# The causal mask of a scan's decays: loaded from DRAM under an adding load, in place of a select on GpSimd over each group's tile

## The chip, the cores and the metric

The kernel runs on one core of one Trainium2 chip. The metric is the time of one execution on the device in microseconds (us). A core has a matrix engine (PE, with its weight loads shown apart as PEld), a vector engine (DVE), a scalar engine (ACT), GpSimd (POOL), and a queue engine without arithmetic (SP). Each engine works through its own list of instructions in order, and an instruction waits on semaphores for what others must have done before it. Loads and stores (DMAs) are issued by SP, ACT or POOL and carried out by 16 DMA engines that they share.

## The reference

One block of a network on 512 tokens of width 1024: an RMS norm, one wide projection, a convolution branch, a state-space branch, gates, an output projection, and a feed-forward part. The change lies in the state-space branch, in the weights by which a token reads earlier ones:

```
a_dt = dt * a                                  # per head, per token
a_cs = cumsum(a_dt)                            # running sums within a chunk
seg  = a_cs[l] - a_cs[s]
decay_in = exp(where(s <= l, seg, -inf))       # causal
cb   = einsum(c_mat, b_mat)                    # per group, l by s
y_diag = einsum(cb, decay_in, x * dt)
```

There are 8 groups of 4 heads (32 heads of width 64). The reference takes chunks of 64 tokens; the kernel works with chunks of 128, so it has 4 chunks, and a group's decays are a tile of 128 partitions (s) by 4 heads x 4 chunks x 128 tokens (l) in float32: 128 x 2048, 1 MB.

## The kernel before

Every large matrix product is made of three float32r passes (`mm3`: high by high, low by high, high by low part), so each strip of weights of 128 x 1024 is loaded (`w_raw`, L194, on SP's queue, tile `raw`), cast to a high part (`w_part`, L202, ACT, `whi`), and given a low part `wlo` in one of two ways: DVE subtracts (L209), or ACT writes the negated high part (L206) and POOL's queue issues an adding load of the same weights onto it (L207, `accum_op=ADD`). Five `raw` and five `whi`/`wlo` buffers exist, so that a strip is loaded several strips ahead of the products that use it.

The state-space branch is a loop over the 8 groups. Iteration g projects x, B and C of group g (`px`, `pB`, `pC` in three banks taken in turn), runs their short convolutions on ACT and DVE (L599, L601, L605), and between these products carries out the scan of group g-1 in steps:

- `s1(g-1)` transposes, scales by dt (`xdt`, L670), and multiplies the decays by C B (L686, DVE, in place in tile `L`)
- `s2(g-1)` makes the states (`pSa`, `pSb`, then `prev`, L698 to L701) and the within-chunk outputs `yd` (L709: 64 small products that read `L`)
- `s3(g-1)` adds the part from earlier chunks (`pYa`, `pYb`, L721), the gate and the norm (L717 to L748)
- `s4` transposes back for the output projection `pso`, whose first four strips' results ACT copies out (L780) and later ones DVE adds up (L782)

Between these, DVE works through the taps of a long convolution (L514, tile `a`; ACT starts each channel block of it, L511), a number of them per step.

Tile `L` of group g+1 is made at the end of iteration g (`make_L`). The running sums of all heads lie in a DRAM tile `scr`; POOL's queue loads the group's 4 x 4 x 128 sums to all 128 partitions (L486, a plain load of 1 MB), POOL's `affine_select` puts -1e30 where l < s (L489), and 16 exponentials on ACT, one per head and chunk with the negated running sum of s as bias, turn it into decays (L496). `L` has two buffers. Group g+1 takes that of group g-1, so its load waits until the products `yd` of group g-1 are done.

A scheduler orders each engine's list from the order of the code and the dependences. Loads of weights keep their order among themselves, and `by_table` keeps the exponentials and the other users of a table of functions in order on ACT.

Of the kernel before, what the change touches and what calls it, by code (L numbers as in the profile page):

```python
# [18 lines left out]
P = 128  # L19
T = 512  # L20
NT = T // P
# [5 lines left out]
G = 8  # L27
HG = H // G
# [142 lines left out]
def block_kernel(ctx: ExitStack, tc: tile.TileContext, x, xT, x0, prm, hp, gp, wf, w, out):  # L171
    nc = tc.nc
# [258 lines left out]
    dec = ssd.tile([P, NT, H], F32, name="dec")  # L431
    cd = ssd.tile([P, NT, H], F32, name="cd")
    scr = dr.tile([H, NT, P], F32, name="scr")

    scratch = ssd.tile([P, 8, CH], F32, tag="y", bufs=2, name="scratch")
    ta, tb, tcx, td, acs, acsT, te = (scratch[:, i, :].rearrange("p (a b) -> p a b", a=NT) for i in range(7))
# [39 lines left out]
    def by_table(ins):  # L476

        if "table" in mark:
            not_before(ins, mark["table"])
        mark["table"] = ins  # L480

    def make_L(g, first=None):
        L = ssd.tile([P, HG, NT, P], F32, tag="L", bufs=2, name=f"L{g}")
        Lf = L.rearrange("p h c l -> p (h c l)")
        src = scr[HG * g : HG * (g + 1)].rearrange("h c l -> (h c l)").partition_broadcast(P)
        load = pool.dma_start(Lf, src)  # L486
        if first:
            not_before(load, first)
        pool.affine_select(  # L489
            out=Lf, in_=Lf, compare_op=ALU.is_ge, fill=-1e30, base=0,  # L490
            pattern=[[0, HG * NT], [1, P]], channel_multiplier=-1,
        )
        for c in range(NT):
            for h in range(HG):
                by_table(
                    act.activation(L[:, h, c, :], L[:, h, c, :], AF.Exp, bias=nacs[:, c, HG * g + h : HG * g + h + 1])  # L496
                )
        return L


    vs, va, taps = [], [], []
# [18 lines left out]
    st = {}  # L520
# [29 lines left out]
    for j in range(NK):  # L550
        if j == EARLY:
            proj_z0()
            time_steps()
        if j == DT2:
            running_sums()
            L = {0: make_L(0)}
        if j == 0:
            three = [glu_tile(n) for n in ("pv0", "pg0", "pv1")]
            ws = [w_get("val", 0), w_get("glu", 0), w_get("val", 1)]
            for k in range(NK):  # L560
                c = slice(k * P, (k + 1) * P)
                for n in range(6 if k < 2 else 3):
                    ps, (wh, wl) = three[n % 3], ws[n % 3]
                    if n < 3:
                        in_order(pe.matmul(ps, wh[:, c], ehi[k], start=k == 0, stop=False))
                        in_order(pe.matmul(ps, wl[:, c], ehi[k], start=False, stop=False))
                    if k > 1 or n > 2:
                        mark["pe"] = in_order(pe.matmul(ps, wh[:, c], elo[k], start=False, stop=k == NK - 1))
            continue
        early = (ehi, elo) if j < EARLY else None  # L570
        pv = three[2] if j == 1 else glu_tile(f"pv{j}")
        if j == 2:
            proj(pv, w_get("val", j), early, slice(0, 3))
            norm_to_all()
            gated(0, *three[:2], True)
            gated(1, *first, True)
            proj(pv, w_get("val", j), early, slice(3, NK))
        elif j > 1:
            proj(pv, w_get("val", j), early)
        pg = glu_tile(f"pg{j}")  # L580
        if j == 1:
            proj(pg, w_get("glu", j), early, slice(0, 4))
            with tc.issue_after(mark["pe"].ins):
                norm_x()
            proj(pg, w_get("glu", j), early, slice(4, NK))
# [199 lines left out]
    for g in range(G):  # L785
        proj_x(g, 0)
        proj_x(g, 1)
        if g % 2 and g > 1:
            s4(g - 2)
        if g:  # L790
            s1(g - 1)
        conv_some((TAPS[g] + 0) // 5 + (TAPS[g] + 1) // 5)
        st[g]["L"] = L.pop(g)
        proj_bc(g, "B")
        if g % 2 and g > 1:
            ssm_out((g - 3) // 2, (0, 1))
        if g:
            s2(g - 1)
        if g % 2 == 0 and g > 1:
            s4(g - 2)  # L800
        conv_some((TAPS[g] + 2) // 5)
        proj_bc(g, "C")
        if g % 2 and g > 1:
            ssm_out((g - 3) // 2, (2, 3))
        if g:
            s3(g - 1)
        conv_some((TAPS[g] + 3) // 5)
        if g == 1:
            proj_z1()
        if g and g % 2 == 0:  # L810
            proj_zz(g)
        if g + 1 < G:
            L[g + 1] = make_L(g + 1, st.pop("lo", None))
        conv_some((TAPS[g] + 4) // 5)


# [986 lines left out]
```

## Time and profile before

| | |
|---|---|
| median of 3 runs | 1017.24 us (1017.21 to 1019.05) |
| span of the profiled execution, first to last instruction | 1016.0 us |
| the median less that span: what lies around it | 1.2 us |
| PE busy | 1007.7 us, 99% of the span |
| DVE, ACT, POOL busy | 847.9, 616.9, 106.7 us |
| moved by DMAs | 155.02 MB, mean 153 GB/s |
| loads of `L` | 8 of 1024 KB, median 7.6 us from issue to landing |
| selects on `L` | 8, some 2.0 us each |

Busy time is the union of the intervals in which an engine had an instruction in flight; matmuls overlap, so a busy PE says that it had no gap, not that each product was quick. The share in brackets is of the span. In the rows by group or in order of time, a bracket at the end holds the engine's idle time just before the row and what ended it; L with a number is a line of the kernel, `out<-in` the tiles written and read.

### The profile page before, as it was taken

To read this page: it belongs to the slowest core of one execution; us is meant where nothing else is said; L and a number is where in the kernel's file an instruction comes from. 1 tells how busy PE (TensorE), PEld (TensorE's weight loads), DVE (VectorE), ACT (ScalarE), POOL (GpSimd) and SP (SyncE) were. 2 spreads that over 40 slices of the span, in tenths; PEclk is the share of its full clock that TensorE was granted. 3 is DMA by queue.
4 is the path that set the end of the run, shared out by engine and by line. 5 is a ranking of instruction groups with operands and counts; after the bars stand their busy time and mean duration, and the time that the engine had idled before them with its cause. 6 is when DMAs were issued, how large, how long until landed. Compare 5 with 4: busy or idle time off the path is not lost.

```text
span 1016.0 us, 15943 instructions
## 1 busy us (share of the span) xinstructions
PE 1007.7 (99%) x6184; PEld 881.7 (87%) x6184; DVE 847.9 (83%) x1233; ACT 616.9 (61%) x1038; POOL 106.7 (11%) x138
## 2 busy tenths in 40 slices
PE   9999999999999999999999999999999999999997
PEld 7898889888888888888888889889999999998886
DVE  7899977868696879678987889788999887899974
ACT  7655775667666746573552685466666566568552
POOL 0101202120121011100110111012000000001001
PEclk9999999999999999999999999999999999999999
DMA  8567635645554465356452355624755555469622
GB/s 302 151 168 218 158 96 145 187 110 144 158 151 117 130 182 151 102 135 163 99 139 69 114 142 165 223 104 118 230 151 160 153 143 146 128 177 295 212 83 83
DMA packets 43803, 155.02 MB, mean 153 GB/s; under 512 B 5072, under 2 KB 6096, under 8 KB 42704
## 3 DMA queue, kind: packets, MB, share of 16 engines
q1 hardware_dynamic: 30672, 105.44, 30.7%
q0 software_dynamic: 11136, 43.00, 21.7%
q10 hardware_dynamic: 1920, 5.57, 1.6%
q8 instruction: 48, 0.79, 0.3%
q14 instruction: 27, 0.22, 0.1%
HBM read 149.73 MB, written 4.26 MB: 152 GB/s over the span
## 4 chain that ended last, share of the span: by engine, by line
PE 87%; DVE 8%; ACT 3%; issue 1%; DMA 1%; SPq 0%; POOL 0%; POOLq 0%; DVEq 0%; ACTq 0%
PE xy L246 4%; PE xy L252 4%; PE xy L248 4%; PE pso L246 3%; PE pso L248 3%; PE pso L252 3%; PE yv L246 2%; PE yv L252 2%; PE yv L248 2%; PE px L246 2%; PE px L252 2%; PE px L248 2%; DVE a L514 2%; PE pz L248 2%; PE pz L252 2%; PE pz L246 2%
## 5 line engine op out<-in xcount | busy, mean ns | idle before, releaser
L514 DVE SCALAR_TENSOR_TENSOR a<-v,prm_t,a 128x511 f32<-128x511 f32 (+15 forms) x240 | 183.8, 769 | 14.3 <-ACT a L511 12.3
L202 ACT CAST whi<-raw 128x1024 fp32r<-128x1024 f32 x99 | 102.6, 1048 | 127.9 <-PE pso L248 36.7
L209 DVE TENSOR_TENSOR wlo<-raw,whi 128x1024 fp32r<-128x1024 f32 x58 | 70.6, 1220 | 32.7 <-ACT whi L202 32.5
L207 POOL DMA_DIRECT2D wlo<-in_w x41 | 36.5, 891 | 369.1 <-ACT wlo L206 171.4
L248 PE MATMUL pz<-wlo,hhi 128*128 128x512 f32 (+2 forms) x160 | 56.2, 351 | 0.2
L252 PE MATMUL pz<-whi,hlo 128*128 128x512 f32 (+2 forms) x160 | 56.1, 352 | 0.0
L246 PE MATMUL pz<-whi,hhi 128*128 128x512 f32 (+2 forms) x160 | 55.4, 353 | 0.0
L246 PE MATMUL px<-hhi,whi 128*128 128x512 f32 x128 | 50.2, 392 | 0.0
L246 PE MATMUL pso<-yh,whi 128*128 128x512 f32 x128 | 50.2, 394 | 0.0
L252 PE MATMUL px<-hhi,wlo 128*128 128x512 f32 x128 | 49.8, 389 | 0.0
L248 PE MATMUL px<-hlo,whi 128*128 128x512 f32 x128 | 49.8, 389 | 0.0
L248 PE MATMUL pso<-yl,whi 128*128 128x512 f32 x128 | 49.8, 390 | 0.0
L252 PE MATMUL pso<-yh,wlo 128*128 128x512 f32 x128 | 49.7, 390 | 0.0
L1189 ACT CAST whi_g<-raw 128x1024 fp32r<-128x1024 f32 x40 | 41.2, 1052 | 10.6 <-PE yv L248 4.9
L601 DVE SCALAR_TENSOR_TENSOR x<-px,prm_t,x 128x511 f32<-128x511 f32 (+2 forms) x48 | 34.7, 743 | 13.9 <-ACT x L599 13.8
L1196 DVE TENSOR_TENSOR wlo_g<-raw,whi_g 128x1024 fp32r<-128x1024 f32 x34 | 41.3, 1221 | 3.5 <-ACT whi_g L1189 3.4
L206 ACT ACTIVATE wlo<-whi 128x1024 fp32r<-128x1024 f32 x41 | 43.3, 1055 | 0.3
L496 ACT ACTIVATE L<-L,nacs 128x128 f32<-128x128 f32 x128 | 38.8, 389 | 0.1
L248 PEld LDWEIGHTS pz<-wlo,hhi 128*128 128x128 f32 x160 | 30.1, 188 | 4.9 <-DVE wlo L209 1.0
L246 PEld LDWEIGHTS pz<-whi,hhi 128*128 128x128 f32 x160 | 30.2, 189 | 3.9
L252 PEld LDWEIGHTS pz<-whi,hlo 128*128 128x128 f32 x160 | 30.1, 188 | 3.7
L1189 ACT CAST chi_g<-raw 128x1024 fp32r<-128x1024 f32 x24 | 24.9, 1053 | 8.8 <-PE yv L248 3.4
(763 smaller groups left out, 3450.7 us busy)
## 6 DMA issues: line engine op xcount, KB each, us to landing
raw<-in_w SPq DMA_DIRECT2D x182, 512.0 KB, 4.5
wlo<-in_w POOLq DMA_DIRECT2D x41, 512.0 KB, 6.8
L<-scr POOLq DMA_DIRECT2D x8, 1024.0 KB, 7.6
wlo_g<-in_w POOLq DMA_DIRECT2D x11, 512.0 KB, 7.0
clo_g<-in_w POOLq DMA_DIRECT2D x6, 512.0 KB, 5.5
pws<-in_w POOLq DMA_DIRECT2D x8, 256.0 KB, 5.9
pw_raws<-in_w SPq DMA_DIRECT2D x4, 512.0 KB, 7.0
xr<-in_x ACTq DMA_DIRECT2D x4, 512.0 KB, 3.9
```

Source lines behind the costliest of these rows:

```text
L202: mark[n, c.start] = act.copy(hi[:, c], src)
L206: act.activation(lo[:, c], hi[:, c].bitcast(F32), AF.Copy, scale=-1.0)
L207: mark["lo"] = pool.dma_start(lo[:, c], w[n][:, c].bitcast(F32R), accum_op=ALU.add)
L209: mark["wlo"] = dve.tensor_tensor(out=lo[:, c], in0=src, in1=hi[:, c].bitcast(F32), op=ALU.subtract)
L246: mark["pe"] = pe.matmul(ps, lh, rh, start=start, stop=False, skip_group_check=more)
L248: pe.matmul(ps, lh, rl, start=False, stop=False, skip_group_check=more)
L252: mark["pe3"] = pe.matmul(ps, ll, rh, start=False, stop=stop, skip_group_check=more)
L496: act.activation(L[:, h, c, :], L[:, h, c, :], AF.Exp, bias=nacs[:, c, HG * g + h : HG * g + h + 1])
L514: return dve.scalar_tensor_tensor(out=va[j][:, d:], in0=vs[j][:, : T - d], scalar=col("dw_w", j * KC + KC - 1 - d), in1=va[j][:, d:], op0= ...
L601: dve.scalar_tensor_tensor(out=a[:, d:], in0=ps[:, : T - d], scalar=col("ssm_w", i * KS + KS - 1 - d), in1=a[:, d:], op0=ALU.mult, op1=ALU ...
L1189: a_ = act.copy(hi, src)
L1196: d_ = dve.tensor_tensor(out=lo, in0=src, in1=hi.bitcast(F32), op=ALU.subtract)
```

## The change

The mask is no longer selected into each group's tile. For group 0, POOL clears the tile, selects -1e30 into it once (`memset` and `affine_select`), and SP's queue stores the result to a new DRAM tile `masked` (1 MB). For every later group SP's queue loads `masked` into the tile (`fill_L`, a plain load of 1 MB). In all 8 groups the load of the running sums from `scr` becomes an adding load onto that tile. Seven selects go; one clearing, one store and seven plain loads come. `fill_L(g + 1)` stands in the code right behind `s2(g-1)`, `fill_L(0)` and `fill_L(1)` around the making of the running sums.

```
+    masked = dr.tile([P, HG * NT * P], F32, name="masked")
+    L = {}
...
-    def make_L(g, first=None):
-        L = ssd.tile([P, HG, NT, P], F32, tag="L", bufs=2, name=f"L{g}")
-        Lf = L.rearrange("p h c l -> p (h c l)")
-        src = scr[HG * g : HG * (g + 1)].rearrange("h c l -> (h c l)").partition_broadcast(P)
-        load = pool.dma_start(Lf, src)
-        if first:
-            not_before(load, first)
+    def fill_L(g):
+        L[g] = ssd.tile([P, HG, NT, P], F32, tag="L", bufs=2, name=f"L{g}")
+        Lf = L[g].rearrange("p h c l -> p (h c l)")
+        if g:
+            nc.sync.dma_start(Lf, masked)
+            return
+        pool.memset(Lf, 0.0)
         pool.affine_select(
             out=Lf, in_=Lf, compare_op=ALU.is_ge, fill=-1e30, base=0,
             pattern=[[0, HG * NT], [1, P]], channel_multiplier=-1,
         )
+        nc.sync.dma_start(masked, Lf)
+
+    def make_L(g, first=None):
+        Lf = L[g].rearrange("p h c l -> p (h c l)")
+        src = scr[HG * g : HG * (g + 1)].rearrange("h c l -> (h c l)").partition_broadcast(P)
+        load = pool.dma_start(Lf, src, accum_op=ALU.add)
+        if first:
+            not_before(load, first)
         for c in range(NT):
             for h in range(HG):
...
         if j == DT2:
+            fill_L(0)
             running_sums()
-            L = {0: make_L(0)}
+            make_L(0)
+            fill_L(1)
...
         if g:
             s2(g - 1)
+            if g + 1 < G:
+                fill_L(g + 1)
...
         if g + 1 < G:
-            L[g + 1] = make_L(g + 1, st.pop("lo", None))
+            make_L(g + 1, st.pop("lo", None))
```

PE's list is the same in both kernels. On the other engines the lists change at each group in the same way; group 4 is shown. On SP's queue before, around the end of group 2's `yd` (tile numbers differ between the two kernels; `raw_2415` before is `raw_2414` after, the strip with which B of group 4 is projected):

```order
L194 DMA raw_2295<-in_w 128x1024 [waits DMAHW1_49,Activation_49]
L194 DMA raw_2330<-in_w 128x1024 [waits DMAHW0_49,DVE_49]
L194 DMA raw_2415<-in_w 128x1024 [waits DMAHW3_49,Activation_49]
L194 DMA raw_2452<-in_w 128x1024 [waits DMAHW2_49,DVE_49]
L194 DMA raw_2486<-in_w 128x1024 [waits DMAHW5_49,Activation_49]
```

And the same place on SP's queue after, where L488 is the load of the mask into the tile of group 4, and PE in its wait is the end of group 2's `yd`:

```order
L194 DMA raw_2292<-in_w 128x1024 [waits DMAHW5_49,Activation_49]
L194 DMA raw_2327<-in_w 128x1024 [waits DMAHW4_49,DVE_49]
L488 DMA L_2407<-masked 128x2048 [waits DMASW5_49,DVE_49,PE_49]
L194 DMA raw_2414<-in_w 128x1024 [waits DMAHW7_49,Activation_49]
L194 DMA raw_2451<-in_w 128x1024 [waits DMAHW6_49,DVE_49]
L194 DMA raw_2485<-in_w 128x1024 [waits DMAHW1_49,Activation_49]
```

The mask's load stands between two loads of weights, so the weights behind it are issued after group 2's `yd`, whatever they wait for themselves. On POOL before, at the same place, the load of the sums, the select behind it, and the adding loads of weights around them:

```order
L207 DMA wlo_2418<-in_w 128x1024 [waits DVE_49,DMASW0_49,PE_49,Activation_49]
L486 DMA L_2556<-scr 128x2048 [waits DVE_49,PE_49]
L489 AFFINE_SELECT L_2556<-L_2556 128x2048 [waits DMASW7_49]
L207 DMA wlo_2489<-in_w 128x1024 [waits DVE_49,DMASW2_49,PE_49,Activation_49]
L207 DMA wlo_2622<-in_w 128x1024 [waits DVE_49,DMASW3_49,PE_49,Activation_49]
```

And on POOL after, where DMAHW3 is the landing of the mask's load:

```order
L207 DMA wlo_2417<-in_w 128x1024 [waits DVE_49,DMASW0_49,PE_49,Activation_49]
L500 DMA L_2407<-scr 128x2048 [waits DMAHW3_49,DVE_49,PE_49]
L207 DMA wlo_2488<-in_w 128x1024 [waits DVE_49,DMASW2_49,PE_49,Activation_49]
L207 DMA wlo_2617<-in_w 128x1024 [waits DMASW1_49,DVE_49,DMASW3_49,PE_49,Activation_49]
L258 TENSOR_SCALAR pm<-ss_2533 128x4 [waits Activation_49]
```

The select is gone and the load of the sums now waits for the mask to have landed. On ACT after, the exponentials of group 4 stand where they stood, between the copies of `pso`, the start of a channel block of the long convolution (L519, L511 before) and two casts of weights; the first of them waits for the adding load (DMASW7) in place of POOL:

```order
L609 ACTIVATE C_2445<-pC_2413,prm_t 128x512 [waits PE_49]
L202 CAST whi_2487<-raw_2414 128x1024 [waits DMAHW4_49]
L206 ACTIVATE wlo_2488<-whi_2487 128x1024 [waits DMASW2_49,Activation_49]
L790 COPY so_1103<-pso_4_2457 128x512 [waits PE_49]
L615 ACTIVATE C_2445<-C_2445 128x512 [waits DVE_49]
L506 ACT_TABLE_LOAD
L506 ACTIVATE L_2407<-L_2407,nacs 128x128 [waits DMASW7_49]
L790 COPY so_1104<-pso_5_2471 128x512 [waits PE_49]
L506 ACTIVATE L_2407<-L_2407,nacs 128x128 x5
L790 COPY so_1105<-pso_6_2492 128x512 [waits PE_49]
L506 ACTIVATE L_2407<-L_2407,nacs 128x128 x5
L519 ACTIVATE a_2552<-v_802,prm_t 128x512
```

One row has moved here: before, the cast of the weights stood ahead of `C<-pC`, now it stands behind it.

More of the change, by code (lines that the diff above doesn't have):

```diff
@@ L492, in make_L @@
         )
+        nc.sync.dma_start(masked, Lf)
[5 more added lines that the diff above has]
+            not_before(load, first)
         for c in range(NT):
             for h in range(HG):
[L495 to L498, printed above, removed]
+                l_ = L[g][:, h, c, :]
+                by_table(act.activation(l_, l_, AF.Exp, bias=nacs[:, c, HG * g + h : HG * g + h + 1]))
     vs, va, taps = [], [], []
@@ L792, in block_kernel @@
         conv_some((TAPS[g] + 0) // 5 + (TAPS[g] + 1) // 5)
-        st[g]["L"] = L.pop(g)
+        st[g]["L"] = L[g]
         proj_bc(g, "B")
```

## The prediction

> **What bounds the kernel now.** I read the page's busy line and chain first, then engine time by stage, then tile `L` and the rows around each load of it. The fences show lines of the page, and one stage and the sum of the scan (by windows: start, end, length, then busy us of each engine).
>
> ```profile
> span 1016.0 us, 15943 instructions
> PE 1007.7 (99%) x6184; PEld 881.7 (87%) x6184; DVE 847.9 (83%) x1233; ACT 616.9 (61%) x1038; POOL 106.7 (11%) x138
> q1 hardware_dynamic: 30672, 105.44, 30.7%
> q0 software_dynamic: 11136, 43.00, 21.7%
> raw<-in_w SPq DMA_DIRECT2D x182, 512.0 KB, 4.5
> ```
>
> ```profile
> 240.00:310.00 70.00, 70.00 (x433) 58.48 (x432) 59.92 (x85) 40.75 (x71) 10.72 (x11) 1.00 0.55 143
> sum 415.00, PE 414.43 PEld 347.21 DVE 332.78 ACT 261.29 POOL 58.78; mean PE 69.07 PEld 57.87 DVE 55.46 ACT 43.55 POOL 9.80
> ```
>
> PE is the bound: in the 415 us from 85 to 500 us, which hold the whole scan, it is idle for 0.57 us, at a granted clock of 1.00. PE's list does not change, so the change can gain at most those 0.57 us there, and it loses whatever makes PE wait. The question is therefore not what the selects cost but whether the new loads land late, and who then holds up PE.
>
> **The change part by part.** The rows of tile `L`, its landing times, and the loads of it that matter below:
>
> ```profile
> L489 POOL TENSOR_SCALAR_AFFINE_SELECT L<-L x8: 2003/2007/2119, 100.2 to 405.9; 128x2048 f32<-128x2048 f32 x8
> DMA to landing us min/median/max: 5.0/7.6/10.5
> 154.26 0.56 POOL L486 DMA_DIRECT2D L<-scr  x1 [1.10 <-PE yd L709]
> 194.34 0.56 POOL L486 DMA_DIRECT2D L<-scr  x1 [0.70 <-PE yd L709]
> 256.69 0.56 POOL L486 DMA_DIRECT2D L<-scr  x1 [2.82 <-PE yd L709]
> 265.67 2.01 POOL L489 TENSOR_SCALAR_AFFINE_SELECT L<-L 128x2048 f32<-128x2048 f32 x1 [8.41 <-DMA L<-scr]
> 359.99 0.57 POOL L486 DMA_DIRECT2D L<-scr  x1 [5.29 <-PE yd L709]
> ```
>
> Each load waits for `yd` two groups earlier. Before, one load (5.0 to 10.5 us) and one select (2.0 us) follow it. After, two loads of 1 MB follow it, one behind the other, since the adding load waits for the landing of the mask's.
>
> *Prices.* No adding load of 1 MB is in the trace, nor a plain one on SP. For the mask's I take the shortest load of `L`, 5.0 us, with the median 7.6 as the other end: the 512 KB loads on SP land in 4.5, and the source is one plain block. For the adding load I use the page's queues: q1, all plain, took 30.7% of 1016.0 us for 105.44 MB, 2.96 us/MB. q0 took 220.5 us for 43.0 MB; without the 8.39 MB of `L` at q1's price (24.8 us), its adding loads come to 195.7/34.6 = 5.65 us/MB. The surplus, 2.7 us/MB, makes 2.8 us on 1 MB: 7.8 us against the shortest load, 10.4 against the median. I take 9.1, half way, as four weight loads that were held back move beside it. From the end of `yd` (0.3 us before POOL's row in each fence: 153.9, 194.0, 256.4, 359.7): 5.0 + 0.3 (POOL's issue) + 9.1 = 14.4 us; ends 13.1 and 18.3.
>
> *Removed selects.* Two shifted products on DVE beside group 4's select, and DVE's next:
>
> ```profile
> 265.79 3.16 DVE L514 SCALAR_TENSOR_TENSOR a<-v,prm_t,a 128x483 f32<-128x483 f32 x2
> L514 DVE SCALAR_TENSOR_TENSOR a<-v,prm_t,a x240: 629/732/2399, 49.5 to 557.2; 128x509 f32<-128x509 f32 x8, 128x507 f32<-128x507 f32 x8, 128x505 f32<-128x505 f32 x8, 128x503 f32<-128x503 f32 x8
> ```
>
> Two at the median would take 1.46 us: the select holds DVE up by 1.7 us, over seven groups 11.9 us of DVE. PE does not wait for DVE there (0.57 us of idle time in all), so 0. The Trainium skill's page "SBUF — State Buffer", section "Who interferes with whom", states that GpSimd shares a port pair with DVE under an exclusive lock; row 265.79 agrees. Taken as the price of the whole change, 11.9 us of DVE over seven groups would be 11.9 us off the span, 1004.1; PE's idle row denies it.
>
> *Group 0.* Clearing, select and store stand early, at about 48 to 58 us, ahead of the first load of sums at 92.95; POOL is 11% busy over the span. 0; a late store would cost weights behind it on SP, as follows.
>
> *SP's queue.* Each of the fills of groups 2 to 7 waits on SP for a `yd`, and the weights behind it wait too. At group 4, SP's row of five weight loads, and ACT around the wait:
>
> ```profile
> 234.23 23.66 SPq L194 DMA_DIRECT2D raw<-in_w  x5
> 261.79 1.05 ACT L202 CAST whi<-raw 128x1024 fp32r<-128x1024 f32 x1 [6.59 <-PE pC L248]
> 265.97 0.63 ACT L605 ACTIVATE C<-C 128x512 f32<-128x512 f32 x1 [0.64 <-DVE C L601]
> 266.62 1.28 ACT L496 ACT_TABLE_LOAD   x1
> 267.91 0.40 ACT L496 ACTIVATE L<-L,nacs 128x128 f32<-128x128 f32 x1
> 268.22 0.57 ACT L780 COPY so<-pso 128x512 f32<-128x512 f32 x1
> 272.40 0.80 ACT L511 ACTIVATE a<-v,prm_t 128x512 f32<-128x512 f32 x1
> 274.75 1.99 ACT L202 CAST whi<-raw 128x1024 fp32r<-128x1024 f32 x2
> ```
>
> The first, issued at 234.23 before, is cast at 261.79. After, it goes out at 256.4, behind the mask: 5.0 us plus its own 0.524 MB x 2.96 = 1.6 give 263.0, 1.2 late (3.8 at the median). ACT has 0.93 us idle between 262 and 268 (busy 5.07), and now waits for the sums in any case, so 0. The other three land by 268 and are cast from 274.75 on: 0. Group 2 (a cast at 158.23 before) and group 6 have the same, with idle time on ACT right behind:
>
> ```profile
> 158.23 1.04 ACT L202 CAST whi<-raw 128x1024 fp32r<-128x1024 f32 x1
> 162.46 0.63 ACT L605 ACTIVATE C<-C 128x512 f32<-128x512 f32 x1 [3.19 <-DVE C L601]
> 369.72 0.63 ACT L605 ACTIVATE C<-C 128x512 f32<-128x512 f32 x1 [1.96 <-DVE C L601]
> ```
>
> By the same sum the cast of group 2 is 2.3 late (153.9 + 6.6 = 160.5), under 3.19: 0; that of group 6, due at 359.7 + 6.6 = 366.3, runs inside the wait for the sums: 0. For group 3 the code's order puts the cast behind others on ACT, so 0 again.
>
> *The adding load, group 4.* Before, ACT was ready for the exponentials at 267.90, when the table was in, and the select had ended at 267.68. After: 256.4 + 14.4 = 270.8, so 2.9 us late (269.5 to 274.7: 1.6 to 6.8). Behind the exponentials on ACT stand copies of `pso`, casts, and `a` at 272.40, for which DVE waits. From there:
>
> ```profile
> 273.23 0.75 DVE L514 SCALAR_TENSOR_TENSOR a<-v,prm_t,a 128x511 f32<-128x511 f32 x1 [4.29 <-ACT a L511]
> 281.38 1.53 DVE L601 SCALAR_TENSOR_TENSOR x<-px,prm_t,x 128x511 f32<-128x511 f32 x2 [0.62 <-ACT x L599]
> 285.54 0.69 DVE L670 TENSOR_TENSOR xdt<-pxT,dtt 128x512 f32<-128x512 f32 x1 [0.17 <-PE pxT L667]
> 301.18 0.42 DVE L701 TENSOR_TENSOR prev<-pSb,ptmp 128x256 f32<-128x256 f32 x1
> 302.33 1.03 PE L721 MATMUL pYa<-prev,C 128*128 128x256 f32 x4
> 273.81 0.58 PE L246 MATMUL px<-hhi,whi 128*128 128x512 f32 x1
> ```
>
> DVE's idle time on that way is 0.62 + 0.17 = 0.8 us, and `pYa` has 0.7 (302.33 less 301.60): 1.5 us of a delay are absorbed, the rest reaches PE. The price is 2.9 - 1.5 = 1.4 us (0.1 to 5.3). The copy at 268.22 frees a bank that `px` takes at 273.81; it has 5.0 us, so it is not the first to bind.
>
> *The other groups.* Where ACT takes up the exponentials, and what it waits for soon after in group 6:
>
> ```profile
> 172.65 0.41 ACT L496 ACTIVATE L<-L,nacs 128x128 f32<-128x128 f32 x1
> 226.87 3.33 ACT L496 ACTIVATE L<-L,nacs 128x128 f32<-128x128 f32 x11
> 371.66 4.80 ACT L496 ACTIVATE L<-L,nacs 128x128 f32<-128x128 f32 x16
> 380.87 0.42 ACT L745 ACTIVATE jk<-y 128x256 f32<-128x256 f32 x1 [2.52 <-DVE y L738]
> ```
>
> Group 2: 153.9 + 14.4 = 168.3 (ends 167.0 and 172.2), ahead of 172.65: 0. Group 3, and with it 5 and 7, whose turn is as far off: 194.0 + 18.3 = 212.3 at worst against 226.87: 0. Group 6: 359.7 + 14.4 = 374.1 against 371.66, 2.4 late, which ACT's idle 2.52 before 380.87 takes up: 0 (at the upper end 378.0, 6.3 late, 3.8 over, of which DVE's small gaps take some: up to 2.5 as an estimate from group 4's 1.5).
>
> *Sum.* 0 (selects) + 0 (group 0) + 0 (SP) + 1.4 (group 4) + 0 (group 6): span 1016.0 + 1.4 = 1017.4 us; with the 1.2 us around it, 1018.6, against the median 1017.24 = 1016.0 + 1.2. That is +0.14%, and about 0.2% (2.03 us) is what a measurement of this kernel can tell from no change.
>
> **The rivals.**
> - *Slower by the adding load.* At the upper price, 18.3 us behind `yd`, group 4 loses 5.3 us: span 1021.3, time 1022.5; with group 6's 2.5, 1025.0. It decides from a delay of 3.5 us on (1.5 absorbed, 2.0 measurable), that is from a landing after 271.4. For it: DMA engines are 97% busy from 256.3 to 262 already:
>
> ```profile
> 256.30:262.00 5.70, 5.70 (x27) 4.74 (x26) 2.44 (x4) 0.21 (x1) 0.56 (x1) 1.00 0.97 264
> 262.00:268.00 6.00, 6.00 (x28) 4.95 (x28) 4.37 (x4) 5.07 (x7) 2.33 (x2) 1.00 0.50 175
> ```
>
>   Against it: they fall to 50% by 268, and the held weight loads are part of those 97%, now behind the mask.
> - *Slower by SP's wait.* If the weights held behind a mask's load land 3.8 us late, ACT's cast at 261.79 is late by that, less 0.9 of idle time and 1.5 absorbed: 1.4 us in a group, in groups 2, 4 and 6 together 4.2: 1021.4. It decides when two of these groups bind (2.8 us). Against it: ACT then waits for `L` anyhow, and the two delays overlap rather than add. The Trainium skill, "DMA: Bandwidth & Descriptors", section "Anatomy of one DMA — SWDGE (gpsimd) path", states that a semaphore wait happens on the issuing sequencer before dispatch, which speaks against this change; no row of before has a wait of such length with weights behind it on SP. Its fit for one transfer (2.0 us plus bytes over 436e3) would make an estimate of 4.4 us for the mask, against the 5.0 measured for the shortest load of `L`, and the sum 1018.0.
> - *Faster.* Seven selects of 2.0 us fewer, and DVE free by 11.9 us. All of PE's idle time in the scan gone makes 1016.7, which would still measure as no change. For more, PE's products themselves would have to be shortened by DVE's relief, which no row shows.
>
> **How the numbers follow.** No measurable change: 0.60, for delays in group 4 up to 3.5 us, with group 6 covered: with the mask at 5.0 us the adding load may then take up to 9.7, which is 1.9 of the 2.6 us between its two ends. Slower by the adding load 0.27, by SP's wait 0.08: together 0.35. Faster 0.05. The range: below 1016.6, the faster rival's bound without the stall; above 1022.0, near the upper price at group 4. Beyond lie group 6 on top and several of SP's waits.
>
> **What the changed profile would show.** Right: PE's busy time unchanged, idle in the scan 1 to 3 us and around 300 us, right behind group 4's delay; the mask's loads 5 to 8 us, the adding loads 8 to 10.5; ACT's wait before group 4's exponentials ended by the load of `L`, 2 to 4 us long; no 3.16 us on DVE near 266; casts near 263. Wrong: PE idle for 3 us or more in front of `pYa`, or for `whi` of a held weight, in several groups; adding loads far above 10 us; or PE's span shorter by more than its 0.57 us of idle time, which would mean that a matmul's duration depends on what DVE and POOL do.

## The result, and the profile after

| | before | after |
|---|---|---|
| median | 1017.23 us (4 runs, 1016.54 to 1019.05) | 1030.65 us (4 runs, 1030.23 to 1031.45) |
| ratio | | 1.0131, 95% interval 1.0117 to 1.0146 |
| span of the profiled execution | 1016.0 us | 1029.0 us |

The change costs 13.4 us. The prediction was 1018.6, with 1016.6 to 1022.0 as its range and "no measurable change" as the likeliest case; the time lies outside the range. The lines of the page after that answer to those shown of before:

```profile
span 1029.0 us, 15948 instructions
PE 1010.3 (98%) x6184; PEld 882.4 (86%) x6184; DVE 840.6 (82%) x1233; ACT 616.5 (60%) x1038; POOL 96.8 (9%) x132
q1 hardware_dynamic: 31824, 113.83, 31.1%
q0 software_dynamic: 11136, 43.00, 23.5%
raw<-in_w SPq DMA_DIRECT2D x182, 512.0 KB, 5.1
L<-scr POOLq DMA_DIRECT2D x8, 1024.0 KB, 11.3
L<-masked SPq DMA_DIRECT2D x7, 1024.0 KB, 5.8
```

The loads of the sums have gone from a median of 7.6 us to 11.3; the mask's loads of 5.8 stand ahead of them. POOL and DVE are less busy (by 9.9 and 7.3 us), as the removed selects promised, and the kernel is slower. By stage (start, end, length, busy us of PE, PEld, DVE, ACT, POOL, granted clock, DMA share, GB/s):

```profile
85.00:140.00 55.00, 52.08 (x224) 42.17 (x223) 44.94 (x64) 33.22 (x51) 5.57 (x7) 0.97 0.65 154
240.00:310.00 70.00, 65.90 (x418) 54.43 (x417) 51.75 (x74) 41.68 (x74) 6.49 (x8) 1.00 0.49 126
310.00:400.00 90.00, 88.60 (x459) 73.19 (x459) 65.50 (x96) 53.12 (x102) 9.79 (x13) 1.00 0.60 166
sum 430.00, PE 419.26 PEld 349.69 DVE 327.51 ACT 261.13 POOL 45.05; mean PE 69.88 PEld 58.28 DVE 54.58 ACT 43.52 POOL 7.51
```

PE is idle for 10.7 us of the 430 from 85 to 515 us; before it was 0.57 of 415. Two stages hold most of it: 2.9 us between 85 and 140, where group 0's decays are made, and 4.1 between 240 and 310, where group 4's are. Read by a landmark that both kernels have, the end of `yd`, the lateness against the kernel before grows in three places: 6.3 us by group 0's `yd` (160.19 against 153.89), 5.9 more from the end of group 2's to that of group 4's (371.44 against 359.62 at the latter), and 1.1 more by group 6's, with one wait of PE of 1.34 us for `prev` at 416.90. Of the 5.9, 4.3 show already at group 3's `yd`, which PE reaches after group 4's exponentials. The tiles of groups 1, 2, 3, 5 and 7 themselves add nothing.

**Group 4**, in order of time after (SP, POOL, ACT, then PE; the bracket is the engine's idle time and what ended it):

```profile
262.27 0.33 SPq L488 DMA_DIRECT2D L<-masked  x1
262.69 7.32 SPq L194 DMA_DIRECT2D raw<-in_w  x6
267.72 0.87 POOL L500 DMA_DIRECT2D L<-scr  x1 [7.91 <-DMA L<-masked]
280.80 0.40 ACT L506 ACTIVATE L<-L,nacs 128x128 f32<-128x128 f32 x1 [7.73 <-DMA L<-scr]
281.73 0.50 PE L246 MATMUL px<-hhi,whi 128*128 128x512 f32 x1 [1.66 <-ACT so L790]
301.36 1.10 PE L707 MATMUL pSa<-xdec,BT 128*128 128x256 f32 x4 [0.88 <-DVE xdec L685]
304.12 2.08 PE L719 MATMUL yd<-xdt,L 128*64 128x64 f32 x64 [1.23 <-DVE L L696]
312.08 0.63 PE L771 MATMUL pyT<-ident,y 128*128 128x128 f32 x4 [1.40 <-DVE prev L711]
```

The mask goes out at the end of `yd`, and five weight loads in the 2.6 us behind it (a sixth, in the same row, follows at 269.68). Four of the five, 2 MB, went out ahead of this `yd` in the kernel before. The mask has landed by 267.1 (4.8 us), the adding load is issued at 267.72, and ACT waits 7.73 us for it. It lands 13.1 us after its issue and 18.6 us after `yd`. What the first 4.3 of those 13.1 us went to can be read in the queues. From 267.7 to 272 us:

```profile
q1 hardware_dynamic: 436, 1.59, 99.1%
```

That is the whole answer for these 4.3 us: the DMA engines are full with plain loads (q1), and no packet of the adding load's queue (q0) moves. The weights that SP had to hold behind the mask's load are let go together, and their packets go first.

**Group 0**, after, in order of time (DVE and POOL near 50 us, then POOL, ACT, DVE and PE):

```profile
50.75 2.91 DVE L522 SCALAR_TENSOR_TENSOR a<-v,prm_t,a 128x510 f32<-128x510 f32 x1
50.77 2.35 POOL L491 TENSOR_SCALAR_AFFINE_SELECT L<-L 128x2048 f32<-128x2048 f32 x1
98.73 1.77 POOL L500 DMA_DIRECT2D L<-scr  x2 [7.16 <-DMA scr<-scratch]
108.96 4.79 ACT L506 ACTIVATE L<-L,nacs 128x128 f32<-128x128 f32 x16 [7.41 <-DMA L<-scr]
113.66 1.05 ACT L206 ACTIVATE wlo<-whi 128x1024 fp32r<-128x1024 f32 x1
115.68 1.22 DVE L209 TENSOR_TENSOR wlo<-raw,whi 128x1024 fp32r<-128x1024 f32 x1 [7.04 <-ACT whi L202]
120.55 0.50 PE L252 MATMUL pB<-hhi,wlo 128*128 128x512 f32 x1 [0.95 <-DMA wlo<-in_w]
127.82 0.47 PE L246 MATMUL pC<-hhi,whi 128*128 128x512 f32 x1 [1.97 <-DVE x L611]
155.72 1.10 PE L707 MATMUL pSa<-xdec,BT 128*128 128x256 f32 x4 [0.98 <-ACT whi L202]
```

The rows of the kernel before that answer to POOL's loads, ACT's exponentials and the `wlo` row beside them:

```profile
92.95 1.11 POOL L486 DMA_DIRECT2D L<-scr  x2 [1.34 <-DMA scr<-scratch]
100.19 1.05 ACT L206 ACTIVATE wlo<-whi 128x1024 fp32r<-128x1024 f32 x1
102.55 4.80 ACT L496 ACTIVATE L<-L,nacs 128x128 f32<-128x128 f32 x16
```

POOL's one select of the changed kernel holds one product of DVE for 2.91 us where its like takes 0.74. DVE has no idle time from there to 92 us, so ACT's `dec`, which waits for it, is at 91.91 instead of 90.27, and with it the four stores of the running sums; they land after 4.4 to 4.9 us instead of 1.5, and the loads of the sums start 5.8 us later. Then the two adding loads take 10.2 and 14.6 us, against 7.2 and 10.5 before. ACT stands still for 7.41 us in front of the exponentials, with the casts behind them that DVE waits for (7.04 us), and DVE's lost time comes out on PE.

Why the stores land late can be read in the queues. They are on ACT's queue (q10), and an adding load of weights on POOL's (q0) was issued at 90.72. In the kernel before, the last of q10's 192 packets started at 92.31 us, and q0's first at 92.32. After, nothing moves from 91.9 to 95.5 us but the adding load (first line), and the stores follow from 95.5 to 98 us (second line):

```profile
q0 software_dynamic: 125, 0.51, 95.4%
q10 hardware_dynamic: 192, 0.07, 11.1%
```

ACT's list has changed here too, which the lists of group 4 do not show. Before, the row L206 at 100.19 stood ahead of the exponentials, and the adding load of weights that needs it was issued at 102.19. After, it stands behind them, at 113.66; that load is issued at 115.11, and PE waits 0.95 us for it. A few casts and one more L206 close behind are rearranged too.

### The profile page after: what moved, and what is told of

Read it like the earlier page. It is cut to its first block, busy times and chain, and to the rows that moved or that the text cites. A ratio compares the mean times of both kernels' runs of the same rounds, so it can differ in the third digit from the quotient of the medians.

```text
span 1029.0 us, 15948 instructions
## 1 busy us (share of the span) xinstructions
PE 1010.3 (98%) x6184; PEld 882.4 (86%) x6184; DVE 840.6 (82%) x1233; ACT 616.5 (60%) x1038; POOL 96.8 (9%) x132
## 3 DMA queue, kind: packets, MB, share of 16 engines
q0 software_dynamic: 11136, 43.00, 23.5%
## 4 chain that ended last, share of the span: by engine, by line
PE 73%; DVE 14%; ACT 6%; DMA 5%; issue 2%; SPq 0%; POOL 0%; ACTq 0%; POOLq 0%; DVEq 0%
DVE a L522 5%; PE xy L246 4%; PE xy L252 4%; PE xy L248 4%; DMA L<-scr 3%; PE yv L248 2%; PE yv L252 2%; PE yv L246 2%; PE pz L246 2%; PE pz L248 2%; PE pz L252 2%; PE pso L246 2%; PE pso L248 2%; PE pso L252 2%; ACT L L506 2%
## 5 line engine op out<-in xcount | busy, mean ns | idle before, releaser
L522 DVE SCALAR_TENSOR_TENSOR a<-v,prm_t,a 128x511 f32<-128x511 f32 (+15 forms) x240 | 176.5, 739 | 24.3 <-ACT a L519 22.3
L506 ACT ACTIVATE L<-L,nacs 128x128 f32<-128x128 f32 x128 | 38.9, 388 | 21.8 <-DMA L<-scr 21.7
L206 ACT ACTIVATE wlo<-whi 128x1024 fp32r<-128x1024 f32 x41 | 43.3, 1055 | 0.3
## 6 DMA issues: line engine op xcount, KB each, us to landing
L<-scr POOLq DMA_DIRECT2D x8, 1024.0 KB, 11.3
```

Source lines behind the costliest of these rows:

```text
L206: act.activation(lo[:, c], hi[:, c].bitcast(F32), AF.Copy, scale=-1.0)
L506: by_table(act.activation(l_, l_, AF.Exp, bias=nacs[:, c, HG * g + h : HG * g + h + 1]))
L522: return dve.scalar_tensor_tensor(out=va[j][:, d:], in0=vs[j][:, : T - d], scalar=col("dw_w", j * KC + KC - 1 - d), in1=va[j][:, d:], op0= ...
```

## The experiments

All ratios are to the kernel before on the same chip. The lateness is that of the end of `yd` of groups 0, 2, 4 and 6 against the kernel before's profile, in us. PE's products are the same in all of these kernels, so it can be read at any of them. Already at 40 us the profiles lie 0.7 us ahead of the kernel before's to 0.4 behind it; where that matters below, the text counts from there and says so.

| kernel | median | ratio (95%) | group 0 | 2 | 4 | 6 |
|---|---|---|---|---|---|---|
| after | 1030.65 | 1.0131 (1.0117 to 1.0146) | 6.3 | 5.9 | 11.8 | 12.9 |
| e1, mask's load on POOL | 1028.86 | 1.0112 (1.0096 to 1.0127) | 5.8 | 5.4 | 11.8 | 12.8 |
| e2, plain load of the sums | 1021.08 | 1.0033 (1.0020 to 1.0046) | 3.0 | 2.7 | 4.0 | 3.5 |
| e3, small mask at 50 us | 1030.51 | 1.0126 (1.0110 to 1.0141) | 5.9 | 5.5 | 11.9 | 13.1 |
| e4, before plus the early select | 1020.13 | 1.0029 (1.0019 to 1.0038) | 1.4 | 1.5 | 1.6 | 1.1 |
| e5, mask made by POOL | 1025.54 | 1.0082 (1.0067 to 1.0097) | 4.7 | 4.8 | 6.6 | 7.4 |
| e6, groups 3, 5, 7 alone | 1019.12 | 1.0025 (1.0007 to 1.0042) | 4.4 | 4.0 | 4.0 | 3.6 |
| e8, groups 2 to 7 | 1026.39 | 1.0092 (1.0069 to 1.0115) | 3.2 | 2.8 | 8.4 | 9.3 |
| e9, group 4 alone | 1025.32 | 1.0086 (1.0060 to 1.0111) | 0.2 | 0.3 | 6.4 | 5.9 |
| e10, mask made at the start | 1027.79 | 1.0106 (1.0090 to 1.0122) | 2.4 | 2.1 | 7.9 | 8.8 |
| e11, 3, 5, 7 alone, mask at the start | 1016.99 | 0.9995 (0.9986 to 1.0004) | -0.7 | -1.1 | -1.0 | -1.5 |

**e1: the mask's load on POOL's queue.**

```
-            nc.sync.dma_start(Lf, masked)
+            (nc.sync if g < 2 else pool).dma_start(Lf, masked)
```

> The changed kernel, but the mask's loads of groups 2 to 7 are issued on POOL's queue, right ahead of the adding load, instead of on SP; SP's weight loads wait for nothing new. Theory A (in the changed kernel the weights that SP held behind the mask's load are released in one go, and the adding load of group 4 sat 4.3 us behind them before its first packet): the adding load of group 4 lands 9 to 10 us after its issue instead of 13.1, its exponentials start 3 to 4 us late instead of 6.9, PE loses 1.5 to 2.5 us there instead of 5.9, group 6 loses nothing; group 0 as in the changed kernel. Time 1025 to 1026 us. Rival B (an adding load of 1 MB takes 11 to 13 us whatever moves beside it): landing and stalls unchanged, 1029 to 1031 us.

Both theories fell. Group 4's two loads on POOL, and ACT's first exponential behind them:

```profile
262.13 0.56 POOL L488 DMA_DIRECT2D L<-masked  x1 [2.81 <-PE yd L719]
271.62 0.86 POOL L500 DMA_DIRECT2D L<-scr  x1 [8.93 <-DVE C L611]
280.79 0.40 ACT L506 ACTIVATE L<-L,nacs 128x128 f32<-128x128 f32 x1 [7.45 <-DMA L<-scr]
```

The second bracket names a product of DVE that ended at about that moment; the load itself waits for the mask's, which landed at 271.2. The adding load, free of weights, took 9.1 us, so it does not take 11 to 13 of itself; but the mask's load now took 9.1 instead of 4.8, and the sums landed 19.0 us after `yd`, as late as in the changed kernel. The DMA engines' queues while the adding load was under way, 271.6 to 280.8 us:

```profile
q0 software_dynamic: 243, 1.45, 86.1%
q1 hardware_dynamic: 13, 0.04, 1.0%
```

With next to no plain load beside it, 1 MB and the half MB of an adding weight load behind it take the engines 9 us. The mask's load, in turn, stands where the plain load of the sums stood in the kernel before, between the same loads of weights, and takes as long as that one did (9.1 us against 8.9). What the mask gained on SP's queue, with the weights held behind it (4.3 us), the sums lost (3.9 us). It is not that the same bytes had to be moved either way: between `yd` and the landing the DMA engines moved 5.8 MB in the changed kernel and 4.0 MB here.

**e2: a plain load of the sums** (it overwrites the mask, so this kernel leaves the mask out and its result is not that of the reference; the bias is another tile, as the expectation says).

```
-        load = pool.dma_start(Lf, src, accum_op=ALU.add)
+        load = pool.dma_start(Lf, src)
```

> The changed kernel with a plain load of the sums in place of the adding one; it overwrites the mask, so the decays of later tokens are not left out, and the bias of the exponentials is another tile of the same shape so that they stay finite. Theory A (two prices add up: the adding load's packets take twice as long, and the held weights go ahead of it): group 4's load still starts some 4 us after its issue and lands after 8.5 to 9.5 us, group 0's after 6 to 7 instead of 10.2; PE gains 3 to 4 us in group 0 and 4 to 5 in group 4: 1021 to 1023 us. Rival B (all of it is the adding): group 4's load lands after 5 to 7.5 us, as in the kernel before, and the loss after group 0 is gone: 1020 to 1021 us, with group 0's late start left.

Theory A holds, at the low end: group 4's plain load, in the same place behind the same weights, landed after 8.5 us instead of 13.1, and the way from group 2's `yd` to group 4's lost 1.3 us instead of 5.9. Over all groups the loads of the sums became shorter by 2.3 to 5.7 us. So the adding alone, on the same transfers, is worth 9.6 us of the 13.4 (1030.65 to 1021.08; the spans, 1029.0 and 1019.4, say the same). Of the 3.5 that are left, little comes from two loads in a row: 3.0 are lost by group 0's `yd`, where the early select and the late stores are those of the changed kernel, and 1.3 at group 4; 0.8 are made up at groups 2 and 6.

**e3: group 0's mask on 128 columns.**

```
-        pool.memset(Lf, 0.0)
-        pool.affine_select(out=Lf, ..., pattern=[[0, HG * NT], [1, P]], ...)
-        nc.sync.dma_start(masked, Lf)
+        if not g:
+            mk = Lf[:, :P]
+            pool.memset(mk, 0.0)
+            pool.affine_select(out=mk, ..., pattern=[[1, P]], ...)
+            nc.sync.dma_start(masked..., mk.unsqueeze(1).to_broadcast([P, HG * NT, P]))
+        nc.sync.dma_start(Lf, masked)
```

> The changed kernel with POOL's clearing and select on 128 of the 2048 columns of group 0's tile (a sixteenth of the work), stored to all 16 blocks of the mask in DRAM, and group 0's tile loaded from it like the others. Theory C (group 0's loss began with the select at 50.8 us, which held up DVE by 2.1 us; by that the four stores of the running sums came behind an adding load of weights and landed 5.8 us later): DVE's shifted product there takes 0.74 us again, the sums land near 92.7 to 93.5, group 0's exponentials start at 103 to 105 us, PE loses 0 to 2 us in group 0 instead of 6.1: 1025 to 1027 us. Rival D (the mask's store and first loads on SP crowd the DMA queues): sums and exponentials as late as in the changed kernel, 1029 to 1031 us.

A miss. DVE was no longer held up (0.73 us), three of the four stores landed after 1.4 to 1.5 us, but the fourth after 3.6, and the loads of the sums were issued at 95.91, against 92.95 before and 98.73 in the changed kernel. Group 0's exponentials came 1.9 us earlier than in the changed kernel, at 107.1, and `yd` only 0.4. The trace says why: from 153.4 to 156.9 us, from PE's wait for `pSa` on, the granted clock is at half:

```profile
153.40:156.90 3.50, 3.06 (x7) 2.52 (x8) 3.50 (x4) 2.09 (x4) 0.00 (x0) 0.51 0.00 0
```

Over the products from 148 us to `yd`, with the same two waits of PE (0.4 and 1.9 us), e3 loses 4.3 us and e10, whose clock stays, 2.8. The stretch at half clock is the 1.5 us between them; nothing behind it takes it up.

**e4: the kernel before with the early clearing and select alone.**

```
+            extra_select()     # memset and affine_select on group 0's tile
             running_sums()
```

> The kernel before, with the changed kernel's early clearing and select on group 0's tile added and nothing else (no mask in DRAM; the plain loads and the select of every group stay). Theory C: DVE is 2 us late from 53 us on, the stores of the sums fall behind the adding load of weights, group 0's load is issued near 98 instead of 92.95 and PE loses 3 to 6 us: 1020 to 1023 us. Rival D (select hidden, the DMAs on SP did it): group 0 within 0.5 us of the kernel before, 1017 us.

The chain is there as theory C has it: DVE's product takes 2.92 us, the stores land after 4.1 to 4.6 us, the loads of the sums go out at 97.67. The price is below the 3 to 6 us that were expected: 2.5 us on the median, and 1.4 at `yd`, or 1.9 from where the profile was at 40 us. Rival D is not needed for this: no DMA was added here. Group 0's exponentials start 4.3 us later against the same products of PE, and cost 1.9. ACT's list is that of the kernel before.

**e5: the mask made by POOL in the tile, from group 2 on.**

```
-        if g:
+            if g == 1:
...
-        nc.sync.dma_start(masked, Lf)
+        if not g:
+            nc.sync.dma_start(masked, Lf)
```

> The changed kernel, but from group 2 on POOL clears and selects the mask into the tile itself (some 4.2 us of POOL) ahead of the adding load; the mask's loads from DRAM are gone. Group 0 as in the changed kernel. Theory A' (after the run with the mask's load on POOL's queue, where the two loads of group 4 took 9.1 and 9.1 us in place of 4.8 and 13.1 and landed at the same time: what the DMA engines have to move between the end of yd and the landing sets the landing, whatever the order): with 1 MB less to move, the sums of group 4 land 13.5 to 15 us after yd instead of 18.6, PE loses 0 to 1.5 us there instead of 5.9: 1024 to 1026 us. Rival B (the adding load takes 11 to 13 us by itself): it lands 16 us or more after yd, 1027 to 1029 us. Rival E (POOL's clearing and select hold DVE up as long as the loads did): landing early, but the time 1027 us or more.

POOL at group 4, from the end of `yd` on, and its select for group 5 with a product of DVE beside it:

```profile
261.22 1.81 POOL L491 MEMSET L<- 128x2048 f32 x1 [2.50 <-PE yd L721]
263.11 2.00 POOL L492 TENSOR_SCALAR_AFFINE_SELECT L<-L 128x2048 f32<-128x2048 f32 x1
265.52 0.88 POOL L502 DMA_DIRECT2D L<-scr  x1 [0.41 <-POOL L L492]
302.74 2.13 POOL L492 TENSOR_SCALAR_AFFINE_SELECT L<-L 128x2048 f32<-128x2048 f32 x1
303.59 1.82 DVE L524 SCALAR_TENSOR_TENSOR a<-v,prm_t,a 128x501 f32<-128x501 f32 x1
```

The time is the one that theory A' gives. Group 4's adding load took 8.7 us, landed 13.0 after `yd` (13.5 to 15 were expected), and the way from group 2's `yd` to group 4's lost 1.8 us instead of 5.9 (0 to 1.5 were expected). Of the 1.8, 1.1 go with POOL's select for group 5: the product of DVE beside it takes 1.82 us instead of 0.73, just ahead of the `prev` that PE waits for. This is rival E, in small. The reason that theory A' names, the bytes to be moved, is not borne out: e1's landing came as late as the changed kernel's with 1.8 MB less. Six loads of 1 MB fewer, and SP's waits with them, are worth 5.1 us with the select kept. The kernel is still 8.0 us slower than the kernel before.

**e6: only groups 3, 5 and 7; e11: the same with the mask stored later.**

```
+    FAR = (3, 5, 7)
...
+        if g in FAR:
+            nc.sync.dma_start(Lf, masked)
...
+        load = pool.dma_start(Lf, src, accum_op=ALU.add) if g in FAR else pool.dma_start(Lf, src)
...
+        if g not in FAR:
+            pool.affine_select(...)
```

> The mask's load and the adding load for groups 3, 5 and 7 alone; groups 0, 1, 2, 4 and 6 by plain load and select as in the kernel before. The mask in DRAM is made from 128 columns of group 1's tile. The prediction's cover for these groups (their exponentials start 22 to 26 us after the select's end): with landings 17 to 19 us after yd nothing waits, and the selects that go free DVE that PE does not wait for: 1016.5 to 1018.5 us. Rival (the weights that SP holds behind the mask's load, or DVE's relief, count): above 1019.5, or below 1015.5.

> The mask's load and the adding load for groups 3, 5 and 7 alone, as in the run with these groups, but with the mask's columns made at the start of the program and stored to DRAM only after 116 us, so that groups 0 and 1 are those of the kernel before. Theory (far groups have cover of 22 us and more; what the run before this lost, it lost ahead of group 1, where the mask's store stood): within 0.2% of the kernel before, 1016.5 to 1018.5 us. Rival (SP's waits in groups 3, 5 and 7 cost): 1019.5 us or more.

e6's median missed its expectation. The mask's store, made from group 1's tile, went out at 96.8 us and group 1's load had to wait for it (issued at 105.5 instead of 93.5). An adding load of weights behind group 1's select was issued at 115.80 instead of 102.19, and PE waited 2.53 us for it; the clock fell to half for 3.5 us behind that wait. All its loss is there; from group 2's `yd` to group 6's it lost nothing. Its runs also scatter more than any other kernel's, 1016.65 to 1024.82 us. With the store out of the way, e11 is level with the kernel before, and PE as busy as there from 85 to 500 us:

```profile
sum 415.00, PE 414.68 PEld 348.38 DVE 328.46 ACT 261.61 POOL 53.55; mean PE 69.11 PEld 58.06 DVE 54.74 ACT 43.60 POOL 8.93
```

Its adding loads took 11.3 to 11.9 us. So a mask's load and an adding load cost nothing in groups 3, 5 and 7, where 22 us and more of cover lie behind them, SP's held weights included; and three selects fewer bring nothing.

**e8: groups 2 to 7** (`FAR = (2, 3, 4, 5, 6, 7)` in e6's edit).

> The change for groups 2 to 7 alone; groups 0 and 1 by plain load and select as in the kernel before, and the mask made from 128 columns of group 1's tile. Theory C' (6.1 us of the changed kernel's loss come from groups 0 and 1 by themselves: the early select, the late stores of the sums and two adding loads): 1024 to 1025.5 us. Rival (the loss at groups 4 and 6 is there only because group 0 left DVE late, or DVE makes up for group 0 later): 1019 to 1021 us, or 1028 and more.

Inconclusive on group 0, since it has e6's late store ahead of group 1 (3.2 us), and the median, 1026.39, lies above what was expected. On the rest it is clear: 5.6 us from group 2 to group 4 and 0.9 to group 6, with group 0 only half as late as in the changed kernel.

**e9: group 4 alone** (`FAR = (4,)`).

> The change for group 4 alone; all other groups by plain load and select. The prediction's rule for the place (delay of the landing against 267.9 us, less 1.5 us) with the landing that the changed kernel showed, 18.6 us after yd: 256.4 + 18.6 = 275.0, 7.1 late, 5.6 us lost: 1022 to 1024 us. Rival (the stalls behind group 4 come from what the groups ahead had lost): a loss of 1 to 3 us, 1018 to 1020.5 us.

ACT's first exponential of group 4, and all waits of PE behind it up to 310 us:

```profile
275.27 0.40 ACT L516 ACTIVATE L<-L,nacs 128x128 f32<-128x128 f32 x1 [7.39 <-DMA L<-scr]
276.20 0.50 PE L246 MATMUL px<-hhi,whi 128*128 128x512 f32 x1 [1.73 <-ACT so L800]
295.83 1.10 PE L717 MATMUL pSa<-xdec,BT 128*128 128x256 f32 x4 [0.88 <-DVE xdec L695]
298.60 2.08 PE L729 MATMUL yd<-xdt,L 128*64 128x64 f32 x64 [1.23 <-DVE L L706]
306.56 0.63 PE L781 MATMUL pyT<-ident,y 128*128 128x128 f32 x4 [1.40 <-DVE prev L721]
```

The load landed at 275.25, where 275.0 was expected, and the way from group 2's `yd` to group 4's lost 6.0 us, where 5.6 was. The same four waits of PE as in the changed kernel follow, of nearly the same length, so they come from group 4's own landing and not from what earlier groups lost. The median, 1025.32, lies above the 1022 to 1024 that were expected, and its 7.8 us are more than the profile's 6.1. The profiled run is the shortest of four, which lie between 1023.83 and 1030.04; what the others lost beyond it is not shown.

**e10: the mask made at the start of the program.**

```
+    mk = ssd.tile([P, GW], F32, tag="jk", name="mk")[:, :P]
+    pool.memset(mk, 0.0)
+    pool.affine_select(out=mk, ..., pattern=[[1, P]], ...)
     x0g = ssd.tile([P, 3 * GW], F32, tag="yo", name="x0g")
```

> The changed kernel, but the mask's 128 columns are made on POOL at the start of the program and stored to the 16 blocks in DRAM at some 48 us; groups 0 and 1 load it at some 67 us. POOL has nothing to do on these tiles near 50 us, and DVE is not held up. Theory C'' (group 0's loss of 6 us has two parts: the sums' stores, which from some 91.2 us on fall behind an adding load of weights, and the two adding loads themselves, 10 and 14.6 us against 7.2 and 10.5 and a select): sums landed by 93 us, group 0's exponentials start 103 to 104.5 us instead of 109, PE loses 0.5 to 2 us in groups 0 and 1, groups 4 and 6 lose 6 to 7 as before: 1024.5 to 1026 us. Rival (ACT's exponentials in front of the casts cost that much however early they start): 1029 to 1031 us.

In part. The mask's store went out at 30.6 us and its loads for groups 0 and 1 at 48.2 and 50.5, earlier than expected. Three stores of the sums landed by 91.6 us, the fourth only at 94.2; the exponentials started at 105.1, and group 0's `yd` is 2.4 us late, or 3.0 from where the profile was at 40 us. Groups 4 and 6 lost 6.8 us (2.1 to 8.8). The median, 1027.8, is above the expected 1024.5 to 1026, and so is the profiled run, 1026.7.

Together they give the loss in parts that nearly add up. For group 0, here is how much later than in the kernel before the first exponential starts, and what is lost by `yd`, both counted from where each profile was at 40 us:

| kernel | exponentials later | lost by `yd` | L206 |
|---|---|---|---|
| after | 6.4 | 6.3 | behind |
| e1 | 5.8 | 5.7 | behind |
| e2 | 3.4 | 3.2 | behind |
| e5 | 5.4 | 5.3 | behind |
| e10 | 3.2 | 3.0 | behind |
| e3 | 4.3 | 5.6, of it 1.5 at half clock | behind |
| e4 | 4.3 | 1.9 | ahead |
| e11 | 2.0 | 0.0 | ahead |

In the changed kernel's order of ACT (L206 behind the exponentials) all but 0.1 or 0.2 us of the delay reaches PE; in that of the kernel before, 2.0 us (e11) and 2.5 us (e4) do not. The adding loads of groups 0 and 1 are 3.1 us (the changed kernel against e2, which differs in them and in the bias alone), and the early select with the late stores 3.3 (against e10): sum 6.4, measured 6.3. The moved row of ACT stands in all three of these kernels, so its share is in both numbers. That it is some 2 us is an estimate from e4 and e11, which also keep the selects of groups 0 and 1; no kernel was run that moves this row alone. (e6, e8 and e9 have a third order and lose ahead of group 1 as well.) From group 2 to group 4: 5.9 (e9 alone, 6.0). Group 6: 1.1. Less the 0.4 made up between the `yd` of groups 1 and 2, that is 12.9 us, of 13.0 in the span.

## Why the prediction was wrong, point by point

- *PE is the bound, and nothing is to be gained.* Right. Seven selects fewer freed DVE (busy 840.6 us instead of 847.9), and no run was faster than the kernel before beyond its interval; e11, with three selects fewer, is level. The row of DVE beside POOL's select was read rightly too, but only for the selects that go.
- *Group 0, "Clearing, select and store stand early", priced at 0.* This is the step that failed first, and in three ways. The price of a select to DVE, 1.7 us, was in the prediction for the seven that were removed; the one that was added, at 50.8 us, cost DVE 2.2 us, at a place where DVE had no idle time up to the running sums (e4: the select alone, 2.5 us of time). The Trainium skill's "SBUF — State Buffer", section "Who interferes with whom", has DVE and GpSimd under an exclusive lock; row 50.75 agrees, and the rule should have been held against the added instruction as well as the removed ones. Group 0's own adding load and group 1's were left out of the sum: only groups 2 to 7 were gone through, though the select's end at 102.24 and the exponentials at 102.55 left ACT 0.3 us of slack there, as little as in group 4. That is 3.1 us (the changed kernel against e2). And ACT's list was compared at group 4 alone: at group 0 the row L206 went behind the exponentials, and the 2 us of delay that cost nothing in e11 were no longer free. In place of 0, group 0 cost 6.3 us.
- *The adding load, taken at 9.1 us.* Mis-sized. The surplus for adding was taken at 2.8 us. As time of the DMA engines that came true: q0's share went from 21.7% of 1016.0 us to 23.5% of 1029.0, 21.3 us more for eight loads, 2.7 each. (Some 1.6 MB of q0's other loads, L951 and L1221, do not add; without them the prediction's sum gives 3.0.) But from issue to landing the surplus between the changed kernel and e2 is 2.3 to 5.7 us, 4.6 in group 4. A quiet adding load takes about what the lower end said (7.8): 7.6 and 7.8 us in e1's groups 3 and 5, 8.4 to 8.7 in e5's groups 4, 5 and 7. But group 4's took 13.1, for 4.3 us of which it stood behind the held weights. The prediction named these four loads and then charged half of the way to the busy end for them; their 2 MB at its own 2.96 us/MB would have been 6.2 us.
- *The landing.* 14.4 us behind `yd` was taken, 18.3 was the upper end; measured 18.6 in group 4 and 17.2 to 18.9 in the others. The rival "slower by the adding load", at 1022.5 to 1025.0, thus was the case that came, at its upper end, and group 0 came on top of it.
- *Group 4's rule, "1.5 us of a delay are absorbed, the rest reaches PE".* Nearly right. e9 was 0.3 us late at group 2's `yd`, so its landing at 275.25 is a delay of 7.0 us against 267.90, and the rule gives 5.5; 6.0 were lost. In the changed kernel, e1, e2, e3, e8 and e10 the loss is above the rule by 0.4 to 0.5 us as well: some 1.0 us is absorbed. The waits were partly others than those named: PE waited first for the copy of `so` that frees `px`'s bank (1.66 us; the prediction gave it 5.0 us of slack, and the delay of 7.0 exceeded them), then for `xdec`, the product on `L` and `prev`.
- *Group 6*: 1.1 us, within the "up to 2.5" that the upper end had. *Groups 3, 5, 7*: 0, right (e11).
- *SP's wait.* The rival as it was put, casts late by held weights, did not show: no wait of PE in the changed kernel's scan is for a weight that SP held. The Trainium skill, "DMA: Bandwidth & Descriptors", section "Anatomy of one DMA — SWDGE (gpsimd) path", has a semaphore's wait happen on the issuing sequencer; rows 262.27 and 262.69 agree, with five weight loads let go in the 2.6 us behind the mask. What they cost was in front of the adding load. Without SP's wait (e1) the mask's own load took 4.3 us longer, so nothing was won.

What stays open is the share of ACT's moved row in group 0's loss, and why the DMA engines finish one queue's packets before they start another's. The stores of the sums, 16 KB each, landed after 1.4 to 1.5 us where their packets moved before the first packet of the adding load of weights that POOL had issued (all four in the kernel before and e9, three in e3, e6, e8, e10 and e11), and after 3.6 to 5.5 us where they did not (all four in the changed kernel, e1, e2, e4 and e5). In the kernel before the last of them started 0.01 us ahead of it, so that kernel had nothing to spare there.

## What to carry to other kernels

A transfer that replaces an instruction has to be priced at the place where it lands, with everything that the new wait lets go at the same moment: here a select of 2 us turned into 1 MB more in a chain of two loads, with 2 MB of held weights in front of the second. Go through every instance of a changed loop, the first above all, and compare the order of each engine's list at each of them; hold an interference found in the profile against the instructions that are added as well as those that go. Where the trace showed cover (22 us in groups 3, 5 and 7), it held here: the change is free there, and brings nothing either.

## What the runs showed of the hardware

- An adding load of 1 MB into the tile took at best 7.6 us and up to 15.2 with others; plain ones of the same size, 4.6 to 5.2 at best. In the traces a packet of 8 KB took 0.63 us when it was added and 0.31 when not, one of 4 KB 0.33 and 0.16 (medians). POOL is also held longer by its issue, 0.87 us against 0.56.
- Packets of one queue waited for those of another twice in these traces: the adding load's for the plain loads of weights (267.7 to 272 us), and the stores' for an adding load (91.9 to 95.5 us).
- In four of the kernels the granted clock fell to half in the scan for some 3.5 us, during or soon after a wait of PE: in the changed kernel at 129 us, and in e3 (twice), e5 and e6. In the changed kernel it came after waits of 0.95 and 1.97 us, and seven matmuls or so started 0.43 us apart instead of 0.23:

```profile
129.00:132.10 3.10, 3.10 (x9) 2.34 (x9) 3.10 (x5) 2.95 (x5) 0.86 (x1) 0.50 0.00 0
132.10:135.00 2.90, 2.90 (x14) 2.39 (x13) 2.87 (x5) 0.94 (x3) 0.00 (x0) 0.95 0.84 124
```

  That is some 1.7 us there, but it does not come on top in group 0's 6.3: PE's next wait, for `pSa`, is 0.98 us, where e1, whose clock stayed, waits 1.92 and pays for as much of its delay. In e3 it came with the last wait, and the time was lost. What sets it off is not shown: e3's clock fell after a wait of 2.11 us at 281.79, and e1's stayed after one of 2.12 at 281.71.
